# Twelve warm-up matmuls, later squares of x, and another order of low parts in a decoder step

## The chip, the cores and the metric

The kernel runs on one core of a Trainium2 chip. A core has a matrix engine (TensorE, PE in the profile; PEld is its weight load), a vector engine (VectorE, DVE), a scalar engine (ScalarE, ACT), a general engine (GpSimd, POOL) and an engine that issues transfers (SyncE, SP); ACT and POOL can issue transfers too. The metric is the device time of one execution in microseconds (us); less is better.

## What is computed

One layer of a decoder trunk, for 256 prompt tokens and 8 x 4 sample tokens (288 columns in all), 2048 channels, in float32:

```python
h = rmsnorm(x, norm1_g)
proj = einsum("btd,de->bte", h, w_in) + b_in
a, gate, z = proj[..., :1024], proj[..., 1024:2048], proj[..., 2048:]
u = a * sigmoid(gate)
c = silu(layernorm(depthwise_causal_conv(u_ext, conv_w, conv_b), ln_g, ln_b))   # 31 taps
d = multiscale_pool(z_ext, pos0)          # windows 2, 4, 8, 16; one for each group of 256 channels
p = einsum("btgc,gce->btge", d, pool_w).reshape(bsz, T, D_POOL) * pool_scale
x = x + einsum("btm,md->btd", concatenate([c, p]), w_out)
f = square(relu(einsum("btd,df->btf", rmsnorm(x, norm2_g), w_ff1)))            # 8192 wide
x = x + einsum("btf,fd->btd", f, w_ff2)
y = rmsnorm(x, norm_f)
```

The new histories of the convolution and of the pooling are outputs as well.

## The kernel before

Channels lie on the 128 partitions, the 288 tokens along the free dimension: `xT` is 16 tiles of 128 x 288. Each weight and each activation is split into a high part (rounded to the matmul's fp32r type) and a low part (what is left), and each product is made of three matmuls: high by high, low by high, high by low.

The weights come from memory as half-tiles of 128 x 1024 (`wr`, six buffers; loads on SP's queue). `split_part` rounds one on ACT to `whi` (line 274) and makes `wlo` in one of three ways: "V" is one subtraction on DVE (line 279); "G" is two subtractions of 128 x 512 on POOL (line 282); "D" writes the negated high part on ACT (line 276) and lets a DMA that POOL issues add the weights to it from memory (line 277). `WAYS` lists the way for each of the four half-tiles of a group of products, in order; "c3" is a convolution group, "p3" a pooling group (the third, of window 16). `whi` and `wlo` have five buffers each. The groups follow in the order of `SEQUENCE` (c0 and c1 together, c2, c3, c4, p3, c5, p2, and so on); a group is 96 matmuls.

The start is written out by hand. SP loads, for each pair of channel tiles, x and the weights of c0 and c1. `warm` is nine matmuls of a constant on TensorE (line 214) that nothing reads. `first_split(k0)` rounds the weights of one pair (`whi`, lines 363 and 370; low part on DVE, line 372) and makes the high parts of x times the norm's gain, `hx` (line 368 on ACT, 366 on DVE for the first; low parts on DVE, line 375). These conversions are traced for all eight pairs first; `squares()` is traced after them, inside the first product group, and fills the tile of `z_all`, which is still free: eight squares of a pair of tiles on ACT (line 417), added up on DVE in two sums (line 419), which are joined (lines 420 and 421).

The inverse root of the mean square isn't needed for the products, only to scale them afterwards. `rsqrt_sums` sums the squares over the partitions by small matmuls into `pt`, at a fixed place in TensorE's order (`between`: behind the low parts of the last pair), then takes roots on a 96 x 3 tile `st` (lines 249 to 256: DVE, one ACT root, DVE). `spread` turns them into a row on all partitions by six small matmul passes, also into `pt`, at a fixed place two tiles of channels into the product group c2 (`between={2: first_rows}`). A MEMSET of `z_all` on POOL (line 534) waits until the small matmuls have read the sums. After that come the scaling of the products, the convolution on DVE (line 460), and all else.

The order on each engine comes from a scheduler that places instructions, by the order in which they were traced and by a simulated time, when the program is built; each engine then works strictly in that order. `tc.issue_after(i)` makes what is traced inside it come behind `i` on that engine and adds no wait.

Of the kernel before, what the change touches and what calls it, by code (L numbers as in the profile page):

```python
# [11 lines left out]
AF = mybir.ActivationFunctionType  # L12
# [57 lines left out]
TURN = "110100" * 4 + "01" * 6 + "1100" * 3  # L70


WAYS = {"c2": "GVGV", "c3": "GDGG", "c4": "GDGD", "p3": "GDDG", "c5": "GDGD", "c": "GGGV", "p": "GVVG", "w0": "VV", "w": "GG", "ff": "VV"}


VEC = (("norm1_g", 16), ("b_in", 24), ("conv_b", 8), ("ln_g", 8), ("ln_b", 8), ("pool_scale", 8), ("norm2_g", 16), ("norm_f", 16))
# [10 lines left out]
def trunk_kernel(ctx: ExitStack, tc: tile.TileContext, io):  # L87
# [3 lines left out]
    nc = tc.nc  # L91
# [32 lines left out]
    def act2(name, **kw):  # L124

        return rows(actp.tile([P, 4, T], F32R, name=nm(name), **(kw or {"tag": "act"})))
# [4 lines left out]
    def ms(name):  # L131
        return msp.tile([P, 2, 512], F32, name=nm(name), tag="ms")

    def f32(t):
        return t.bitcast(F32)
# [15 lines left out]
    xT = const.tile([P, KT, T], F32, name="xT")  # L151
# [4 lines left out]
    def v(key, j):  # L156
        return vec[:, OFF[key] + j : OFF[key] + j + 1]
# [24 lines left out]
    def by_pair(t):  # L182
        return t[:].rearrange("p (i k) c -> p i k c", i=2)
# [26 lines left out]

    load_table(AF.Sqrt, ones[:, 0:1])
    warm = ms("warm")
    for j in range(9):
        nc.tensor.matmul(warm[:, 0, 0:P], ones, ones, start=True, stop=True)
    ident = const.tile([TB, TB], F32, name="ident", padded_shape=[TB, TB + 40])
    make_identity(nc, ident)
# [51 lines left out]
    def split_part(raw, src, hi, lo, way):  # L268

        nc.scalar.copy(hi, raw)  # L274
        if way == "D":
            nc.scalar.activation(lo, f32(hi), AF.Copy, scale=-1.0)
            nc.gpsimd.dma_start(lo, src, accum_op=ALU.add)
        elif way == "V":
            nc.vector.tensor_tensor(lo, raw, f32(hi), op=ALU.subtract)  # L279
        else:  # L280
            for j in range(0, raw.shape[1], 2):
                nc.gpsimd.tensor_tensor(lo[:, j : j + 2, :], raw[:, j : j + 2, :], f32(hi[:, j : j + 2, :]), op=ALU.subtract)  # L282

    def spl():
        return [wspl.tile([P, 4, 256], F32R, name=nm("w" + part), tag="w" + part) for part in ("hi", "lo")]
# [4 lines left out]
    def split(halves, stage="ff"):  # L290

        parts = []
        for raw, src in halves:
            turns[stage] = turns.get(stage, -1) + 1
            parts.append(spl())
            ways = WAYS.get(stage) or WAYS[stage[0]]
            split_part(raw, src, *parts[-1], ways[turns[stage] % len(ways)])
# [53 lines left out]
    def halves(x2):  # L351

        return [(x2[0][:, m, :], x2[1][:, m, :]) for m in range(2)]


    hx, firsts = [], []

    def first_split(k0):
        firsts.append([by_pair(t) for t in spl()])
        raw, hi, lo = raws[k0 // 2], *firsts[k0 // 2]  # L360
        blocks = [slice(i, i + 1) for i in range(2)] if k0 < 4 else [slice(0, 2)]
        hx.extend(halves(act2("hx")))
        nc.scalar.copy(hi[:, blocks[0]], raw[:, blocks[0]])  # L363
        for k in range(k0, k0 + 2):
            if k == 0:
                nc.vector.tensor_scalar(hx[k][0], xT[:, k, :], v("norm1_g", k), None, op0=ALU.mult)  # L366
            else:
                nc.scalar.activation(hx[k][0], xT[:, k, :], AF.Copy, scale=v("norm1_g", k))  # L368
        for b in blocks[1:]:
            nc.scalar.copy(hi[:, b], raw[:, b])  # L370
        for b in blocks:
            nc.vector.tensor_tensor(lo[:, b], raw[:, b], f32(hi[:, b]), op=ALU.subtract)  # L372
        for k in (k0 + 1, k0):
            hh, hl = hx[k]
            nc.vector.scalar_tensor_tensor(out=hl, in0=xT[:, k, :], scalar=v("norm1_g", k), in1=f32(hh), op0=ALU.mult, op1=ALU.subtract)  # L375

    for k in range(0, KT, 2):
        if k >= 12:
            first_load(k)
        first_split(k)  # L380
# [29 lines left out]
    def squares():  # L410

        nc.scalar.copy(scratch[:, :, :, 0:1], f32(firsts[2][0])[:, 1, 1, 0:10].rearrange("p (n k t) -> p n k t", n=5, t=1))
        for q in range(8):
            xq = xT[:, 2 * q : 2 * q + 2, :]
            a = q // 4
            dst = scratch[:, 2 + q % 3] if q % 4 else tot[a]
            nc.scalar.activation(dst, xq, AF.Square)
            if q % 4:
                nc.vector.tensor_tensor(tot[a], tot[a], dst, op=ALU.add)
        nc.vector.tensor_tensor(tot[0], tot[0], tot[1], op=ALU.add)  # L420
        nc.vector.tensor_tensor(tot[0][:, 0, :], tot[0][:, 0, :], tot[0][:, 1, :], op=ALU.add)
        return [tot[0][:, 0, :]]
# [100 lines left out]
    def first_sums():  # L523
        diag.append(rsqrt_sums(squares(), 1.0 / D, AF.Sigmoid))
        return diag[0][2]
# [96 lines left out]
    for g in range(8):  # L622
# [17 lines left out]
        for m, (ah, al) in enumerate(a2):  # L640
            k = 2 * g + m
# [29 lines left out]
    for ch in range(DFF // FCH):  # L671
# [19 lines left out]
        for g in range(8):  # L691
# [5 lines left out]
            for m in range(2):  # L697
                k = 2 * g + m
# [103 lines left out]
```

## Time and profile before

| | us |
|---|---|
| median of 3 runs (lowest to highest) | 1083.59 (1083.45 to 1083.73) |
| the profiled execution's own time | 1083.32 |
| its span, first to last instruction | 1081.2 |
| TensorE busy | 1069.8 |
| DVE busy | 636.8 |
| ACT busy | 477.6 |
| POOL busy | 174.6 |

The profile is of one execution. The span is shorter than the time of that execution by 2.1 us, which lie around it. Rows of the order of time read: start in us, duration in us, engine, line, operation, tile written and tiles read, shapes, count; in brackets the engine's idle time before and what ended it. Rows of waits read: who waited, for whom, us in total, times, longest.

### The profile page before, as it was taken

The numbers are of one execution on the slowest core, as the hardware profiler recorded it, in microseconds if no ns is written. First come the engines' busy times: TensorE is split into PE (matmuls) and PEld (weight loads), VectorE is DVE, ScalarE is ACT, GpSimd is POOL, SyncE is SP. The second block draws the span as 40 slices with busy tenths as digits, with TensorE's granted clock in tenths as the row PEclk, the third lists the DMA queues.
The fourth block names the chain that finished last, engine by engine and source line by source line (L and its number), as shares of the span: only waits on it lengthen the run. The fifth ranks groups of instructions, "written<-read, shape, count | busy, mean of one in ns | idle before, by whom it ended". The sixth has DMA issues, their size and how long they took to land.

```text
span 1081.2 us, 19573 instructions
## 1 busy us (share of the span) xinstructions
PE 1069.8 (99%) x8198; PEld 1068.7 (99%) x8198; DVE 636.8 (59%) x818; ACT 477.6 (44%) x585; POOL 174.6 (16%) x180
## 2 busy tenths in 40 slices
PE   9999999999999999999999999999999999999996
PEld 9999999999999999999999999999999999999996
DVE  7899999787754544444554444555544445554553
ACT  8654445565544433334443333444433334444441
POOL 0878979512000000000000000000000000000001
PEclk9999999999999999999999999999999999999998
DMA  9896468555555555555555555555555555555522
GB/s 327 281 272 184 140 187 250 172 170 170 166 173 164 171 173 165 170 171 164 172 173 162 172 168 168 171 173 163 173 170 165 172 173 163 172 170 165 172 79 88
DMA packets 58296, 190.71 MB, mean 176 GB/s; under 512 B 6240, under 2 KB 11232, under 8 KB 58208
## 3 DMA queue, kind: packets, MB, share of 16 engines
q1 hardware_dynamic: 56336, 184.35, 54.5%
q0 software_dynamic: 1008, 3.67, 1.9%
q8 instruction: 64, 1.05, 0.4%
q10 hardware_dynamic: 864, 1.44, 0.4%
q14 instruction: 24, 0.20, 0.1%
HBM read 185.16 MB, written 4.28 MB: 175 GB/s over the span
## 4 chain that ended last, share of the span: by engine, by line
PE 76%; issue 20%; DMA 2%; DVE 1%; ACT 0%; POOL 0%; SPq 0%; POOLq 0%; DVEq 0%
PE ac L305 75%; DMA wr<-in_w 1%; PE pp L305 1%; DMA u_all<-in_hist_c 0%; DVE wlo L279 0%; POOL xT L738 0%; PE pt L305 0%; ACT whi L363 0%; DVE hx L375 0%; DVE st L255 0%; DVE wlo L372 0%; PE pmean L305 0%; ACT hx L368 0%; SPq L191 0%; POOLq L788 0%
## 5 line engine op out<-in xcount | busy, mean ns | idle before, releaser
L274 ACT CAST whi<-wr 128x1024 fp32r<-128x1024 f32 (+1 forms) x332 | 346.5, 1044 | 553.6 <-PE ac L305 540.6
L279 DVE TENSOR_TENSOR wlo<-wr,whi 128x1024 fp32r<-128x1024 f32 x288 | 353.6, 1228 | 346.0 <-ACT whi L274 346.0
L305 PE MATMUL ac<-ax,whi 128*128 128x288 f32 x2048 | 351.0, 292 | 0.0
L305 PE MATMUL ac<-fx,whi 128*128 128x288 f32 x2048 | 350.2, 292 | 0.0
L305 PEld LDWEIGHTS ac<-ax,whi 128*128 128x128 f32 x2048 | 296.0, 187 | 0.0
L305 PEld LDWEIGHTS ac<-fx,whi 128*128 128x128 f32 x2048 | 295.6, 187 | 0.0
L305 PE MATMUL ac<-ax,wlo 128*128 128x288 f32 x1024 | 217.3, 292 | 0.0
L305 PE MATMUL ac<-fx,wlo 128*128 128x288 f32 x1024 | 216.4, 292 | 0.0
L305 PEld LDWEIGHTS ac<-ax,wlo 128*128 128x128 f32 x1024 | 162.6, 187 | 0.0
L305 PEld LDWEIGHTS ac<-fx,wlo 128*128 128x128 f32 x1024 | 162.2, 187 | 0.0
L305 PE MATMUL ac<-hx,whi 128*128 128x288 f32 x768 | 131.1, 294 | 1.4 <-DVE hx L366 1.4
L738 POOL TENSOR_TENSOR xT<-xT,rf 128x288 f32<-128x288 f32 x4 | 3.1, 796 | 800.1 <-ACT rf L742 800.1
L305 PEld LDWEIGHTS ac<-hx,whi 128*128 128x128 f32 x768 | 111.8, 189 | 1.6 <-ACT hx L368 1.6
L282 POOL TENSOR_TENSOR wlo<-wr,whi 128x512 fp32r<-128x512 f32 x74 | 101.5, 1420 | 35.7 <-ACT whi L274 34.6
L460 DVE SCALAR_TENSOR_TENSOR pc<-u_all,vec,pc 128x256 f32<-128x256 f32 x232 | 99.4, 481 | 1.9 <-ACT pc L457 0.7
L305 PE MATMUL ac<-hx,wlo 128*128 128x288 f32 x384 | 80.1, 294 | 0.0
L305 PEld LDWEIGHTS ac<-hx,wlo 128*128 128x128 f32 x384 | 60.9, 189 | 0.1
L305 PE MATMUL ac<-dx,whi 128*128 128x288 f32 x256 | 46.9, 294 | 0.0
L305 PE MATMUL ac<-mx,whi 128*128 128x288 f32 x256 | 44.6, 292 | 0.0
L682 DVE SCALAR_TENSOR_TENSOR t<-ac,r 128x576 f32<-128x576 f32 x32 | 24.2, 758 | 25.3 <-PE ac L305 25.3
L305 PEld LDWEIGHTS ac<-dx,whi 128*128 128x128 f32 x256 | 38.4, 188 | 0.1
L305 PEld LDWEIGHTS ac<-mx,whi 128*128 128x128 f32 x256 | 37.4, 187 | 0.0
(133 smaller groups left out, 535.2 us busy)
## 6 DMA issues: line engine op xcount, KB each, us to landing
wr<-in_w SPq DMA_DIRECT2D x335, 512.0 KB, 3.8
wlo<-in_w POOLq DMA_DIRECT2D x7, 512.0 KB, 8.2
xT<-in_xT SPq DMA_DIRECT2D x8, 288.0 KB, 7.7
wr<-in_w SPq DMA_DIRECT2D x5, 256.0 KB, 3.7
out_u_out<-u_all SPq DMA_DIRECT2D x1, 1208.0 KB, 9.1
u_all<-in_hist_c SPq DMA_DIRECT2D x8, 136.0 KB, 5.2
out_z_out<-z_all SPq DMA_DIRECT2D x1, 668.0 KB, 9.9
z_all<-in_hist_p SPq DMA_DIRECT2D x4, 152.0 KB, 6.9
```

Of the source, the lines that this page charges most:

```text
L274: nc.scalar.copy(hi, raw)
L279: nc.vector.tensor_tensor(lo, raw, f32(hi), op=ALU.subtract)
L282: nc.gpsimd.tensor_tensor(lo[:, j : j + 2, :], raw[:, j : j + 2, :], f32(hi[:, j : j + 2, :]), op=ALU.subtract)
L305: last = nc.tensor.matmul(*args, **kw)
L460: nc.vector.scalar_tensor_tensor(out=dst, in0=up[:, w : w + SEQ], scalar=cwv[:, w : w + 1], in1=pc, op0=ALU.mult, op1=ALU.add)
L682: nc.vector.scalar_tensor_tensor(out=t, in0=bk[:, :, :T], scalar=0.0, in1=both(rows2[0]), op0=ALU.max, op1=ALU.mult)
L738: eng.tensor_tensor(xk, xk, r[:, None, :].to_broadcast([P, n, T]), op=ALU.mult)
```

## The change

Three edits. Twelve warm-up matmuls instead of nine. The activations that make `hx` for the tiles 1 to 15 are kept in a list, and each square is issued behind one of them: the squares of pairs 0 to 3 behind tile 9's, that of pair 4 behind tile 11's, of pair 5 behind tile 13's, of pairs 6 and 7 behind tile 15's. In the pooling group of window 16 the third half-tile's low part is made on POOL and the fourth's by the accumulating DMA, where it was the other way round.

```diff
-WAYS = {"c2": "GVGV", "c3": "GDGG", "c4": "GDGD", "p3": "GDDG", "c5": "GDGD", "c": "GGGV", "p": "GVVG", "w0": "VV", "w": "GG", "ff": "VV"}
+WAYS = {"c2": "GVGV", "c3": "GDGG", "c4": "GDGD", "p3": "GDGD", "c5": "GDGD", "c": "GGGV", "p": "GVVG", "w0": "VV", "w": "GG", "ff": "VV"}
...
-    for j in range(9):
+    for j in range(12):
         nc.tensor.matmul(warm[:, 0, 0:P], ones, ones, start=True, stop=True)
...
-    hx, firsts = [], []
+    hx, firsts, scaled = [], [], []
...
-                nc.scalar.activation(hx[k][0], xT[:, k, :], AF.Copy, scale=v("norm1_g", k))
+                scaled.append(nc.scalar.activation(hx[k][0], xT[:, k, :], AF.Copy, scale=v("norm1_g", k)))
...
-            nc.scalar.activation(dst, xq, AF.Square)
+            with tc.issue_after(scaled[2 * min(max(q + 1, 4), 7)].ins):
+                nc.scalar.activation(dst, xq, AF.Square)
```

## The prediction

> **What bounds the kernel now.** I read the page first, then TensorE's waits, its pace by stretches, and last the instructions of the first 36 us in order of time with the chain of waits beside them.
>
> ```profile
> span 1081.2 us, 19573 instructions
> PE 1069.8 (99%) x8198; PEld 1068.7 (99%) x8198; DVE 636.8 (59%) x818; ACT 477.6 (44%) x585; POOL 174.6 (16%) x180
> ```
>
> TensorE (PE) is busy for 1069.8 of 1081.2 us, so only what moves its first and its few idle moments can move the end. The list of its waits is short:
>
> ```profile
> PE ac L305 <- DVE hx L366: 1.4, 1, 1.4
> PE warm L214 <- DVE cst L229: 1.0, 1, 1.0
> ```
>
> ```profile
> PEld pt L305 <- DVE st L256: 0.3, 1, 0.3
> ```
>
> The warm-ups start at 1.0 us, there is a hole of 1.4 us ahead of the first real product, and 0.3 us are lost where the weight load of the tile `pt` (the spreading of the inverse roots) waits for the vector engine (DVE). Those are the idle moments; the rest is pace, in this table of stretches (stretch, length, TensorE busy, instructions):
>
> ```profile
> 6.60:9.68 3.08, 3.07 (x13) 1.00 1.05 407
> 9.68:30.00 20.32, 20.32 (x156) 1.00 1.01 363
> ```
>
> The same 288-column product comes every 237 ns (3.08/13) at first, and every 130 ns (20.32/156) after 9.68 us. The view's clock column says 1.00 in both, so the pace shows the slow clock and the column doesn't.
>
> From 30 to 36 us the order of time reads:
>
> ```profile
> 27.90 3.95 POOL L282 TENSOR_TENSOR wlo<-wr,whi 128x512 fp32r<-128x512 f32 x2 [25.59 <-ACT whi L274]
> ...
> 28.48 0.75 DVE L420 TENSOR_TENSOR z_all<-z_all 128x576 f32<-128x576 f32 x1
> ...
> 29.27 1.43 DVE L421 TENSOR_TENSOR z_all<-z_all 128x288 f32<-128x288 f32 x1
> ...
> 30.63 2.31 DVE L279 TENSOR_TENSOR wlo<-wr,whi 128x1024 fp32r<-128x1024 f32 x1
> ...
> 32.22 0.59 PE L305 MATMUL pt<-ones,z_all 128*96 128x1 f32 x6
> 32.53 0.20 POOL L534 MEMSET z_all<- 128x120 f32 x1 [0.68 <-PE pt L305]
> ...
> 32.69 2.65 POOL L282 TENSOR_TENSOR wlo<-wr,whi 128x512 fp32r<-128x512 f32 x2
> 32.86 0.15 DVE L249 TENSOR_SCALAR st<-pt 96x3 f32<-96x3 f32 x1
> ...
> 33.49 0.61 DVE L254 TENSOR_TENSOR st<-st 96x3 f32<-96x3 f32 x1
> ...
> 34.14 1.22 DVE L255 SCALAR_TENSOR_TENSOR st<-st 96x3 f32<-96x3 f32 x1
> 35.39 0.16 DVE L256 SCALAR_TENSOR_TENSOR st<-st 96x3 f32<-96x3 f32 x1
> ...
> 35.61 0.91 PE L305 MATMUL pt<-ident,st 96*128 96x96 f32 x6
> ```
>
> The last sum of squares (L421) ends at 30.70 and TensorE takes it only at 32.22: 1.5 us of slack there. But the three-column arithmetic behind it (L249 to L256) begins at 32.86, when the half-tile subtraction L279 ends, and lasts to 35.55; TensorE is there 0.3 us before. DVE and GpSimd (POOL) take turns: L255 works on 96x3 elements, takes 1.22 us, and ends at 35.36, when POOL's two subtractions end (32.69 + 2.65 = 35.34); L421 and L279 are stretched while POOL's earlier pair (27.90 to 31.85) runs. The chain of waits passes through the same rows, not through TensorE. So up to 35.6 us the end is set by DVE and POOL; TensorE is a close second.
>
> The Trainium skill, page "SBUF — State Buffer", section "Who interferes with whom", says that a DVE instruction with two SBUF inputs and a GpSimd one that reads SBUF exclude each other for the whole instruction. The trace agrees (L255, 1.22 us, ends with POOL). By that rule a TensorE that runs ahead gains nothing here: the spreading stays at 35.6 us.
>
> **The change part by part.**
>
> ```profile
> 1.04 4.21 PE L214 MATMUL warm<-ones 128*128 128x128 f32 x18 [1.04 <-DVE cst L229]
> ...
> 6.61 1.30 PE L305 MATMUL ac<-hx,whi 128*128 128x288 f32 x4 [1.36 <-DVE hx L366]
> ...
> 10.05 0.61 ACT L370 CAST whi<-wr 128x512 fp32r<-128x512 f32 x1
> ...
> 10.73 1.76 PE L305 MATMUL ac<-hx,whi 128*128 128x288 f32 x12
> ...
> 13.59 2.41 ACT L417 ACTIVATE z_all<-xT 128x576 f32<-128x576 f32 x4
> ...
> 14.88 2.49 DVE L419 TENSOR_TENSOR z_all<-z_all 128x576 f32<-128x576 f32 x3 [0.17 <-ACT z_all L417]
> ...
> 15.90 1.04 ACT L363 CAST whi<-wr 128x1024 fp32r<-128x1024 f32 x1
> ...
> 17.29 1.22 DVE L372 TENSOR_TENSOR wlo<-wr,whi 128x1024 fp32r<-128x1024 f32 x1
> ...
> 18.68 1.21 PE L305 MATMUL ac<-hx,wlo 128*128 128x288 f32 x8
> ...
> 25.84 1.04 ACT L363 CAST whi<-wr 128x1024 fp32r<-128x1024 f32 x1
> ...
> 27.35 1.22 DVE L372 TENSOR_TENSOR wlo<-wr,whi 128x1024 fp32r<-128x1024 f32 x1
> ```
>
> Warm-ups. Nine are 18 passes in 4.21 us, 0.234 us each; three more are six passes, 1.4 us, so they end at 6.65 where nine ended at 5.25. The first real product waits for DVE until 6.61. Cost: 0 to 0.04 us, and I take 0. Their gain: TensorE works almost without a hole from 1.04 on. At best the slow pace is over before 6.61: 13 products at 130 instead of 237 ns are 1.4 us. Not all of it can be kept: the second block of the next pair's weights is rounded until 10.66 (L370), its products were due at 10.73 + 8 x 0.13 = 11.8 (four of the 12 close the pair before, four use the first block), so the lead is cut to 11.8 - 10.7 = 1.1 us. At worst the pace changes at 9.68 as now, lead 0. The pace changed 3.1 us after the hole's end, and the new stretch without hole is over 5 us long by 6.61, so I am nearer the upper end: a lead of 1.1 us after pair two.
>
> The Trainium skill, page "TensorE: Matmul & The Clock Gate", section "What's actually happening", has the clock released by a busy window of about 3.4 us at a free-running phase. The trace agrees as far as it goes (slow for 3.1 us after a hole of 1.4 us). By that rule, as an estimate, the release falls between 4.5 and 7.9 us with twelve warm-ups, and if TensorE alone counted the time would be 1083.32 - 1.1 = 1082.2 us.
>
> Squares. Four squares (L417, 2.41 us) run on ScalarE (ACT) from 13.59 to 16.0, ahead of the rounding of the weights of channels 6 and 7 (15.90). Their low half is ready at 17.29 + 1.22 = 18.51 and used at 18.68: 0.17 us of slack, so without the move the lead would be lost here. Behind the change the rounding can start when its weights land:
>
> ```profile
> L187 SPq DMA_DIRECT2D wr<-in_w x1: 614/614/614, 5.4 to 5.4; - x1
> ...
> DMA to landing us min/median/max: 8.1/8.1/8.1
> ```
>
> That is 5.4 + 8.1 = 13.5, so it moves 2.3 us forward and its low half on DVE to 14.7, ready by 15.9, against a use at 18.68 - 1.1 = 17.6. The four squares run at about 15.4 to 17.7, and each conversion up to channels 14 and 15 comes one square (0.6 us) sooner, since one square fewer stands before it. Two squares then stand together before the last rounding, which stays at 25.84: the same ACT work lies before it. DVE is without idle time from 14.88; its work up to L420 is the same, with the additions behind instead of before the first low half. What is bought: the 0.17 us in the row of 14.88, at most; what can be lost: about 0.1 us for each addition that follows directly on another (2.49 us for three, 0.83 each; a single one at 0.75). I take -0.1 us, between -0.2 and +0.4. The DMA queues issue the same transfers in the same order; what SyncE (SP) issues behind a buffer's release comes 0 to 2.3 us sooner, into a DMA system already at 1.01 of its 16 engines in the table, so I count nothing for it.
>
> Third pooling group. Its third half-tile goes from the accumulating DMA to POOL, its fourth from POOL to the DMA. No instruction is added.
>
> ```profile
> 65.94 0.88 POOL L277 DMA_DIRECT2D wlo<-in_w  x1
> 68.78 0.87 POOL L277 DMA_DIRECT2D wlo<-in_w  x1 [1.96 <-ACT wlo L276]
> 70.64 2.54 POOL L282 TENSOR_TENSOR wlo<-wr,whi 128x512 fp32r<-128x512 f32 x2 [0.99 <-ACT whi L274]
> ```
>
> ```profile
> 69.50 1.05 ACT L274 CAST whi<-wr 128x1024 fp32r<-128x1024 f32 x1 [0.29 <-issue]
> ```
>
> The first fence is POOL's order of time, the second ACT's, the next the landing of the transfer of 68.78, the last TensorE's.
>
> ```profile
> DMA to landing us min/median/max: 10.0/10.0/10.0
> ```
>
> ```profile
> 78.36 0.68 PE L305 MATMUL ac<-hx,whi 128*128 128x288 f32 x4
> 78.88 0.52 PE L305 MATMUL ac<-hx,wlo 128*128 128x288 f32 x2
> ```
>
> The transfer issued at 68.78 lands at 78.8, and the products with that low part start at 78.88 though two steps of 0.13 us behind 78.49 would be due at 78.75: 0.1 us lost. On POOL that half takes 2.54 us from about 67.5 (3.1 us, 24 products, before the fourth's 70.64), eight us early. The fourth half is due 3.1 us behind the third, at 82.0; its DMA can issue at about 71.7 (rounding from 69.5, two ACT steps of 1.05, as in the third half) and lands at 81.7 even with the longest delay seen. Gain 0.1 us; bounds: 0.1 us gain, and a loss of 0.5 us if its landing slips by another microsecond. The raw tile of the third half is held 2.6 us longer, that of the fourth given back as much sooner; two loads on SP's queue change by that, for weights of the group after next.
>
> The sum, against the profiled execution's own 1083.32 us: the lead of 1.1 us stops at the spreading (0); the DVE chain -0.1; the pooling group -0.1; 1083.1 us. That execution lies 0.27 us under the median of 1083.59, so against the median this is -0.5 us, -0.04%, inside the 0.2% (2.2 us) that a measurement of this kernel can tell from no change.
>
> **The rivals.** (1) The lead goes through. The scheduler writes each engine's order anew; if L279 comes behind L249 to L256, these start when `pt` ends, 32.81 - 1.1 = 31.7, and last without POOL's turns about 1.6 us (2.7 less the 0.5 and 1.05 us by which L254 and L255 exceed 0.16). TensorE then binds: 1.1 + 0.3 + 0.1, or 1081.9; half of it, 1082.6, where one POOL turn stays. For it: L421 is ready at 30.70, before TensorE's new 31.1. Against: L279's inputs are ready long before, and it fills DVE's wait for `pt`. (2) The sums come late. Each square has a fixed earliest place now, and none by which it must be done. If four of them fall behind the rounding at 25.84 and two more roundings after it, the last ends near 32, L421 near 34, `pt` at 34.6, and the arithmetic with POOL's two turns (which wait for `pt` through the MEMSET) ends near 37.5 instead of 35.55: 1085.2, and 1086 or more with a DMA late behind it. It decides from where L421 ends after 31.1. For it: the squares stand behind all conversions in the program. Against: in the trace one fits after each conversion. (3) The pace doesn't change sooner: the lead is 0, the spreading is at 35.5 all the same, 1083.1 to 1083.3; it can't be told from the forecast by the time.
>
> **How the numbers follow.** Forecast together with (3): 0.55, with its own range 1082.8 to 1083.7 (+-0.4 of the DVE chain, 0.1 of the pooling group, and the 0.27 between profile and median). (1): 0.27, 1081.9 to 1082.8, and 0.02 of it beyond 0.2%. (2): 0.18, 1083.8 to 1086.5, a third of it beyond 1085.8. The range 1081.9 to 1085.0 leaves out 0.02 below and about 0.1 above. Faster by over 0.2%: 0.02; slower: 0.06; the same: 0.92.
>
> **What would show it.** Warm-ups: 24 passes, and the stretch 6.60 to 9.68 with more than 13 products. Squares: the rounding of 15.90 near 13.6, four squares behind 15.4, L420 still near 28.4. Spreading: TensorE's wait for L256 grown from 0.3 to over 1 us with its start at 35.4 to 35.6 is the forecast; a start at 34.2 and no wait is (1); a wait at `pt` for L421 is (2). Pooling group: no 0.1 us before the low part at 78.8. A new TensorE wait anywhere after 40 us, or a reordering on DVE around L279, would make the forecast wrong.

## The result and the profile after

| | before | after |
|---|---|---|
| median of 11 runs, us (lowest to highest) | 1083.73 (1082.75 to 1084.17) | 1085.98 (1084.88 to 1087.34) |
| ratio, 95% interval | | 1.0022 (1.0014 to 1.0029) |
| the profiled execution, us | 1083.32 | 1085.98 |

The kernel became slower by 0.22%. The forecast was 1083.1 us, no measurable difference; the measured time lies 1.0 us above the upper end of its range. From the page of the changed kernel, then TensorE's list of waits (who, for whom, us in total, times, longest):

```profile
span 1084.1 us, 19586 instructions
...
PE 1070.7 (99%) x8204; PEld 1068.6 (99%) x8204; DVE 638.6 (59%) x818; ACT 477.0 (44%) x585; POOL 175.4 (16%) x180
```

```profile
...
PE pp L305 <- ACT dx L502: 0.7, 1, 0.7
PE pp L305 <- DVE dx L503: 0.5, 1, 0.5
PE ac L305 <- DVE u_all L449: 0.4, 1, 0.4
PE pt L305 <- DVE st L256: 0.2, 1, 0.2
PE pt L305 <- DVE z_all L422: 0.2, 1, 0.2
```

Left out are the holes at the start, 1.2 and 1.0 us, and 0.2 us at the end. The first three shown are new: 1.6 us of TensorE idle (line numbers behind 417 are one higher than before). The last, 0.2 us for the sums, is new too and lies at the start. TensorE's order of time shows where:

```profile
159.68 0.42 PE L305 MATMUL ac<-hx,whi 128*128 128x288 f32 x2
160.77 0.54 PE L305 MATMUL pp<-dx,whi 128*128 128x288 f32 x2 [0.66 <-ACT dx L502]
...
162.11 0.80 PE L305 MATMUL pp<-dx,whi 128*128 128x288 f32 x4 [0.54 <-DVE dx L503]
...
173.42 0.37 PE L305 MATMUL ac<-dx,whi 128*128 128x288 f32 x1 [0.41 <-DVE u_all L449]
```

`pp` are the products of the pooling group p1, `dx` is its input, split into high and low parts. That is 125 us behind the start that the squares edit touches. The list counts from the modelled end of the product before; from the start of one product to the start of the next, the three waits cost 0.8, 0.7 and 0.6 us above a step of 0.13 us, 2.1 us in all. The table of stretches counts TensorE's products; first two rows of before, then the same two of after:

```profile
60.00:80.00 20.00, 20.00 (x155) 1.00 1.00 275
...
150.00:175.00 25.00, 25.00 (x194) 1.00 0.85 235
```

```profile
60.00:80.00 20.00, 19.92 (x150) 1.00 0.99 271
...
150.00:175.00 25.00, 23.39 (x174) 1.00 0.76 207
```

Twenty products at 0.13 us are missing around the three waits (2.6 us), and five from 60 to 80 us (0.65 us; behind a hole of 0.1 us at 62.7 us, where the weight load waits for an accumulating DMA, products come every 133.3 ns instead of 130.0). The start gained 0.8 us in these two profiles (the spreading at 34.82 against 35.61). That sums to 2.5 us, where the spans differ by 2.9.

At the start the change did what it says. After, in order of time, and the first of the two stretches that the prediction had shown of before:

```profile
1.04 4.33 PE L214 MATMUL warm<-ones 128*128 128x128 f32 x24 [1.04 <-DVE cst L229]
...
12.81 1.05 ACT L363 CAST whi<-wr 128x1024 fp32r<-128x1024 f32 x1
...
14.63 2.40 ACT L418 ACTIVATE z_all<-xT 128x576 f32<-128x576 f32 x4
...
29.59 1.43 DVE L422 TENSOR_TENSOR z_all<-z_all 128x288 f32<-128x288 f32 x1
30.94 1.21 DVE L279 TENSOR_TENSOR wlo<-wr,whi 128x1024 fp32r<-128x1024 f32 x1
...
34.82 0.91 PE L305 MATMUL pt<-ident,st 96*128 96x96 f32 x6 [0.25 <-DVE st L256]
```

```profile
6.60:9.68 3.08, 3.08 (x24) 1.00 1.06 407
```

Twenty-four products instead of 13 from 6.60 to 9.68: the slow pace was over before the first real product. The rounding of the weights of channels 6 and 7 is at 12.81 instead of 15.90, the four squares follow at 14.63. Nothing there is late.

### The profile page after: what moved, and what is told of

Its sections match the earlier page's. It is cut to its first block, busy times and chain, and to the rows that moved or that the text cites. A ratio compares the mean times of both kernels' runs of the same rounds, so it can differ in the third digit from the quotient of the medians.

```text
span 1084.1 us, 19586 instructions
## 1 busy us (share of the span) xinstructions
PE 1070.7 (99%) x8204; PEld 1068.6 (99%) x8204; DVE 638.6 (59%) x818; ACT 477.0 (44%) x585; POOL 175.4 (16%) x180
## 3 DMA queue, kind: packets, MB, share of 16 engines
q8 instruction: 64, 1.05, 0.4%
## 4 chain that ended last, share of the span: by engine, by line
PE 66%; issue 21%; DVE 6%; POOL 4%; DMA 2%; ACT 1%; POOLq 0%; SPq 0%; DVEq 0%
PE ac L305 66%; DVE pc L461 3%; POOL wlo L282 2%; POOL s L492 1%; DMA wr<-in_w 1%; DMA wlo<-in_w 1%; DVE wlo L279 1%; POOL prd L464 0%; ACT z_all L418 0%; DVE d L497 0%; ACT hx L368 0%; DVE c L466 0%; ACT whi L363 0%; DVE dx L503 0%; POOL xT L739 0%
## 5 line engine op out<-in xcount | busy, mean ns | idle before, releaser
L279 DVE TENSOR_TENSOR wlo<-wr,whi 128x1024 fp32r<-128x1024 f32 x288 | 352.8, 1225 | 346.2 <-ACT whi L274 346.2
L282 POOL TENSOR_TENSOR wlo<-wr,whi 128x512 fp32r<-128x512 f32 x74 | 102.2, 1431 | 33.8 <-ACT whi L274 33.7
L461 DVE SCALAR_TENSOR_TENSOR pc<-u_all,vec,pc 128x256 f32<-128x256 f32 x232 | 99.1, 481 | 3.5 <-ACT pc L458 2.6
```

Of the source, the lines that this page charges most:

```text
L461: nc.vector.scalar_tensor_tensor(out=dst, in0=up[:, w : w + SEQ], scalar=cwv[:, w : w + 1], in1=pc, op0=ALU.mult, op1=ALU.add)
```

## The experiments

All ratios are to the kernel before, run on the same chip. The kernels came in five groups; before measured 1083.16 us beside e1 to e4, 1083.47 beside e5 to e8, 1083.38 beside e9 to e12, 1083.33 beside e13 to e16, and 1083.35 beside e17 and e18.

### Which edit, and by what: e1 to e4

The program's written orders, compared: the warm-ups change only TensorE's own first rows, the swap of low parts a few places on ACT and POOL, but the squares edit gives DVE, ACT, POOL and SP another order from 36 to about 165 us too. e1, e2 and e3 make one edit each; e4 makes all three and holds those four engines behind 36 us to the order that they have without the squares edit, by edges without a wait (lists cut):

```diff
+    keep = {
+        "DVE": "645 646 677 647 648 718",
...
+    }
+    traced = {i.name: i for i in nc.cur_bb.bb.instructions}
+    for order in keep.values():
+        order = [traced["I-" + n] for n in order.split()]
+        for first, then in zip(order, order[1:]):
+            tc.add_manual_dep(then, first.name, mybir.DependencyInfo(mybir.DependencyClass.NoSync, mybir.DependencyReason.DATA), reason="keep")
```

> The later squares alone, nine warm-ups, old order of the third pooling group's low parts. Before, on the same chip, is about 1083.7 us. Theory A (the later squares shift the scheduler's simulated times, so that DVE, ACT and POOL get another order behind 36 us, and TensorE waits at 160 to 173 us): 1085 to 1087 us, with waits of about 0.5 to 1 us at 160 and at 173 us. Theory B (TensorE, 0.8 us ahead, runs into low parts and pooling results that are not ready): no lead without the early clock, 1083.3 to 1084.2 us and none of those waits. Theory C (the exchanged low parts cost it): 1083.3 to 1084.2 us.

> Twelve warm-ups alone. Its order on every engine but TensorE is that of before. All three theories: no 2 us loss. Theories A and C: 1083.0 to 1083.8 us, as the lead is lost where the low part for channels 6 and 7 is ready only at 18.5 us, and none of the waits at 160 to 173 us. Theory B: if any lead lives past 36 us, waits of that size at 160 to 173 us, up to 1084.5 us.

> The exchanged low parts of the third pooling group alone. Theories A and B: 1083.4 to 1083.8 us, TensorE's 0.1 us before the low part at 78.8 us gone. Theory C: 1085 us or more, with TensorE waits behind 60 us.

> All three edits, but DVE, ACT, POOL and SP are held to the order of before behind the start (from about 36 us on; the start up to there is that of the changed kernel). Theory A: the lead of 0.8 us at the spreading stays and the waits at 160 to 173 us go: 1082.4 to 1083.3 us, faster than before. Theory B: the lead is the same, so are the waits: 1085 to 1087 us. Theory C: 1085 us or more.

| kernel | median, us | ratio (95%) |
|---|---|---|
| e1, squares alone | 1085.97 | 1.0031 (1.0019 to 1.0042) |
| e2, warm-ups alone | 1082.73 | 0.9995 (0.9986 to 1.0004) |
| e3, low parts alone | 1083.38 | 1.0001 (0.9992 to 1.0010) |
| e4, all three, old order behind 36 us | 1083.12 | 0.9998 (0.9989 to 1.0007) |

The squares edit carries the loss, and the order that it brings behind 36 us carries it: with that held, the waits at 159 to 173 us are gone. e2 came out 0.3 us below what was expected: its profile loses only 0.2 us at the low part for channels 6 and 7. e4 wasn't faster than before although the start was in its profile; its pace gives a reason (e8 below).

### Is the order enough, and which part: e5 to e8

e5 is before with the new order behind 36 us. e6 and e7 are the changed kernel with a part held: e6 from 100 us, e7 from 36 to 100 us. e8 is e4 with one more edit:

```diff
-            conv_pair(i, conv_products(i, classes=TURN if i == 5 else "", **(dict(gets=ahead(1), between={12: lambda: pool_products(1)}) if i == 7 else {})))
+            conv_pair(i, conv_products(i, classes=TURN if i in (4, 5) else "", **(dict(gets=ahead(1), between={12: lambda: pool_products(1)}) if i == 7 else {})))
```

> The kernel before with none of the three edits, but with DVE, ACT, POOL and SP behind 36 us held to the order in which the scheduler wrote them for the squares-only kernel. Theory A (the order behind the start costs the 2 to 3 us, the squares' own place costs nothing): 1085 to 1086.5 us, and TensorE waits of some 0.9, 0.8 and 0.7 us near 159, 160.5 and 172 us. Rival (the squares at their new places cost it, through a later start or a transfer that they push): 1083 us as before, no such waits. Squares stay at 13.6 to 16 us either way.

> All three edits, with only the order behind about 100 us held to that of the kernel without the squares edit; from 36 to 100 us the scheduler's new order stays. If the order of the second pooling group's chain on DVE, behind 100 us, is what is late (theory A, narrowed): no TensorE waits at 159 to 173 us and 1082.3 to 1083.4 us. Rival (DVE falls behind between 36 and 100 us, through the taps put ahead of pooling steps there): the waits stay, 1085 to 1086 us. It also has no wait near 50 us if the early place of the accumulating transfer's issue is what avoids it, and so TensorE's fast pace until 60 us.

> All three edits, with only the order from 36 to 100 us held to the old one; behind 100 us the order is what the scheduler then gives, which is neither of the two others. If the late order decides and this one is like the squares kernel's: 1084.5 to 1086 us with waits at 159 to 173 us. If the early order decides: 1082.5 to 1083.5 us, no such waits. A wait of 0.2 us near 50 us, as with all held.

> All three edits with the whole order behind 36 us held to the old one, and the product classes of group c4 taken in the turning order that c5 has. If a short TensorE wait flips the pace from 130.0 to 133.3 ns a product and the turning order flips it back: 130 ns from about 60 us on instead of 133.3 until 84 us, that is 0.5 to 0.7 us less than with the old classes, 1082.4 to 1082.7 us. Rival (the slow pace of those stretches belongs to the groups, or to chance): 133.3 ns until 84 us again and 1083.1 us. If the turning order makes c4 wait for its low parts, a new wait near 62 us and up to 0.5 us more.

e5: 1085.79 us, 1.0023 (1.0013 to 1.0032), with the waits. The order alone is enough. Where the squares stand costs nothing that can be told (e4 has them late).

e6: 1086.17 us, 1.0024 (1.0013 to 1.0034), against the expectation. But its waits are others. The longest in TensorE's list, then the order of time on POOL and DVE:

```profile
PE ac L305 <- DVE dx L515: 1.3, 1, 1.3
```

```profile
162.78 3.53 POOL L282 TENSOR_TENSOR wlo<-wr,whi 128x512 fp32r<-128x512 f32 x2 [0.30 <-ACT whi L274]
166.28 0.34 POOL L500 TENSOR_TENSOR d<-s,z_all 128x64 f32<-128x64 f32 x1
167.35 0.76 DVE L503 TENSOR_TENSOR dx<-d,dx 128x576 fp32r<-128x576 f32 x1 [2.22 <-ACT dx L502]
```

The old order was held on POOL only up to the instruction before L500 of the last pooling group. Left free, that one fell behind two subtractions of 3.5 us. e16, below, tests this.

e7: 1084.41 us, 1.0010 (1.0001 to 1.0019), between what the two theories gave. It has no wait at 159 us, but the order that the scheduler then gave has one of 0.2 us at 110 us, and behind it TensorE's slower pace: 480 products from 108 to 172 us where e4 and e8 have 494. This third order tells little about the first two.

e8: 1082.71 us, 0.9992 (0.9983 to 1.0001). Pace of e4, then of e8, by the same stretch:

```profile
48.00:84.00 36.00, 36.00 (x272) 1.00 0.93 253
```

```profile
48.00:84.00 36.00, 36.00 (x277) 1.00 0.93 253
```

Five products more in 36 us, 0.65 us. e4's steps are 133.3 ns long behind a short wait at 50 us and until the group that has the turning order, 130.0 ns elsewhere; in e8 c4 has that order and the pace is back from 66 us on. The medians differ less clearly than the profiles: both intervals hold 1.0.

### A theory that fell: two steps of ACT, e9 to e11

Between 36 and 60 us DVE waits longer for ACT in the new order. e5's list of DVE's waits from 36 to 60 us:

```profile
DVE u_all L448 <- ACT tg L446: 2.2, 1, 2.2
DVE pc L460 <- ACT pc L457: 1.7, 2, 1.0
```

Before has 1.2 and 0.7 there. ACT does the negated high part of c3's second half ahead of the sigmoids `tg`, and two conversions ahead of `pc`. I took these 1.9 us for the source of the lateness at 158 us, since it is as large. e9 puts both back in the changed kernel, e10 the first alone, e11 puts both forward in before; all other places are held.

```diff
 ACT, e9 and e10:
-round, negate, tg, tg
+round, tg, tg, negate
 ACT, e9 alone, in two places:
-round, pc
+pc, round
```

> All three edits and the order of the changed kernel on every engine, except for two places on ACT: the negated high part of c3's second half stands behind the two sigmoids of c2 again (with its accumulating transfer behind POOL's two products prd, as before), and two conversions stand behind the first taps' ACT step pc again instead of ahead of it. Theory A2 (DVE's waits for ACT between 36 and 60 us grow from 2.5 to 4.4 us through these two, DVE has no idle time to make that up in, and the second pooling group's chain is 1.9 us late at 158 us): DVE's waits there back to about 2.5 us, no TensorE waits of 0.7 to 1 us at 159 to 173 us, 1082.3 to 1083.5 us. Rival (DVE's own new order behind 44 us costs it): waits stay, 1085 to 1086 us.

> As the kernel with both steps put back, but only the negation (and its transfer) is moved back; the two conversions stay ahead of pc. By theory A2 DVE's waits from 36 to 60 us are about 3.2 us (4.4 less 1.1), the chain at 158 us is 0.7 us late instead of 1.9, and as the first wait of 0.95 us came from a lateness of 1.9 about 1.0 of it is slack: no wait or one under 0.3 us at 159 us, 1082.5 to 1084.3 us. If the negation isn't the larger part: 1085 us and more.

> The kernel before with its own order on every engine and none of the three edits, except that the negation (with its transfer) is put ahead of the sigmoids and the two conversions ahead of pc. Theory A2: these alone are enough, DVE's waits from 36 to 60 us grow to about 4.4 us, TensorE waits of some 0.7 to 1 us come up at 159 to 173 us, 1084.8 to 1086 us. Rival (it takes DVE's new order too): 1083 to 1084 us and no such waits.

e9: 1085.59 us, 1.0020 (1.0012 to 1.0029). e10: 1085.65 us, 1.0022 (1.0013 to 1.0031). e11: 1083.70 us, 1.0004 (0.9995 to 1.0012). The theory falls on all three: back, they mend nothing; forward, they cost nothing. In e11 DVE does wait 2.2 and 1.2 us there, and TensorE has no wait behind it. The equal size was chance.

### A version with the two harmless edits: e12

```diff
-    for j in range(9):
+    for j in range(12):
...
-classes=TURN if i == 5 else ""
+classes=TURN if i in (4, 5) else ""
```

> The kernel before with twelve warm-up matmuls and the turning order of the product classes in c4 as well as in c5; squares and low parts as before. No TensorE wait at 159 to 173 us; 130 ns a product wherever the kernel with the warm-ups alone has it. Expected 1082.4 to 1082.8 us, that is no more than 0.1 us from the warm-ups alone, since that profile shows no slow stretch before 84 us; if the unprofiled executions often have the wait near 79 us that the profile before has, 0.1 to 0.3 us less.

1083.26 us, 1.0000 (0.9991 to 1.0009); 0.5 us above what was expected. TensorE in its profile, in order of time:

```profile
16.84 1.33 PE L305 MATMUL ac<-hx,whi 128*128 128x288 f32 x8 [0.22 <-ACT whi L363]
18.40 0.81 PE L305 MATMUL ac<-hx,wlo 128*128 128x288 f32 x4 [0.23 <-DVE wlo L372]
```

Without the squares edit TensorE, when it runs ahead, waits for the weights of channels 6 and 7. That is the wait that the squares edit takes away.

### Where DVE meets POOL: e13 to e16

Before and after are level at 117.7 us, where both start the same subtraction on DVE (117.80 and 117.67). Twenty us on, after is 3.2 us behind. DVE and POOL of before, in order of time (d, dx: inputs of the pooling group p2; L279 and L282: the low parts of weights on DVE and on POOL; tz: the start of p1's chain):

```profile
127.70 0.69 DVE L496 SCALAR_TENSOR_TENSOR d<-s,z_all 128x512 f32<-128x512 f32 x1 [0.96 <-POOL s L495]
...
129.25 2.21 POOL L463 TENSOR_TENSOR prd<-u_all,vec 128x992 f32<-128x992 f32 x1
...
131.08 1.00 DVE L502 TENSOR_TENSOR dx<-d,dx 128x576 fp32r<-128x576 f32 x1
...
135.88 1.22 DVE L279 TENSOR_TENSOR wlo<-wr,whi 128x1024 fp32r<-128x1024 f32 x1
...
137.80 0.75 DVE L482 TENSOR_TENSOR tz<-ac,rb 128x576 f32<-128x576 f32 x1
138.01 2.54 POOL L282 TENSOR_TENSOR wlo<-wr,whi 128x512 fp32r<-128x512 f32 x2 [2.47 <-ACT whi L274]
```

And after:

```profile
124.68 3.00 POOL L282 TENSOR_TENSOR wlo<-wr,whi 128x512 fp32r<-128x512 f32 x2
124.77 1.75 DVE L497 SCALAR_TENSOR_TENSOR d<-s,z_all 128x512 f32<-128x512 f32 x1 [1.16 <-POOL s L496]
...
130.19 2.21 POOL L464 TENSOR_TENSOR prd<-u_all,vec 128x992 f32<-128x992 f32 x1 [1.24 <-DVE u_all L449]
130.42 2.60 DVE L503 TENSOR_TENSOR dx<-d,dx 128x576 fp32r<-128x576 f32 x1
...
137.91 3.52 POOL L282 TENSOR_TENSOR wlo<-wr,whi 128x512 fp32r<-128x512 f32 x2 [2.50 <-ACT whi L274]
138.77 1.51 DVE L279 TENSOR_TENSOR wlo<-wr,whi 128x1024 fp32r<-128x1024 f32 x1
140.99 0.74 DVE L483 TENSOR_TENSOR tz<-ac,rb 128x576 f32<-128x576 f32 x1
```

DVE's `d` is 1.06 us longer beside POOL's subtractions, `dx` 1.6 us longer, since it meets POOL's `prd` from its start and not only in its last 0.4 us. There is no more work in them. `d` and `dx` read two tensors in SBUF. The Trainium skill, page "SBUF — State Buffer", section "Who interferes with whom", says that such a DVE instruction and a GpSimd one that reads SBUF exclude each other, and that issue order decides who blocks. The traces agree: `dx` ends 0.62 us behind the end of `prd` in after (133.02 against 132.40) and in before (132.08 against 131.46) alike. Another `dx` of the same size, with POOL idle beside it, takes 0.74 us (at 161.31 us in after).

e13 moves `dx` alone, behind five taps. e14 also gives the 11 DVE instructions ahead of it and POOL's division `s` and sum the old places. e15 puts those new places into before. e16 is e6 with the old order held to about 200 us. (tap: one multiply-add of the convolution, L461; scale: products times the inverse root, L445; subtract: a low part of weights, L279 or L282.)

```diff
 DVE, e13 and e14:
-dx, tap, tap, tap, tap, tap
+tap, tap, tap, tap, tap, dx
 DVE, e14:
-d, tap, scale, tap, subtract, scale, tap, tap, u_all, u_all, tap
+tap, tap, tap, scale, tap, scale, subtract, tap, d, u_all, u_all
 POOL, e14:
-s, s, sum_c, divide, subtract, subtract
+sum_c, s, s, subtract, subtract, divide
```

> All three edits and the changed kernel's order everywhere, except for one DVE instruction: the subtraction dx of the pooling group p2 (at 130.4 us, 2.6 us long beside POOL's prd) stands behind the next five taps. Theory A3 (DVE loses 2.7 us between 117 and 155 us because three kinds of its two-input instructions meet POOL's): dx takes 0.7 to 1.0 us, the chain of the next pooling group comes 1.6 us sooner, of TensorE's waits at 159 to 173 us (0.82, 0.71 and 0.58 us above a step) at most 0.3 us in all is left, 1082.8 to 1084.0 us. Rival (the taps' own order costs it): all waits stay, 1085.5 to 1086.5 us.

> As the kernel with dx moved, and besides d, the taps around it and POOL's last division s of that group in the old order, in all 12 DVE and 3 POOL places between 120 and 134 us. Theory A3: d back from 1.75 to 0.7 us, dx at 1.0, no TensorE wait at 159 to 173 us, 1082.3 to 1083.5 us. Rival (the loss is spread over the whole new order, of which this stretch is a tenth): waits of 0.3 us and more stay, 1084.5 us or more.

> The kernel before, none of the three edits, its own order on every engine except for those 12 DVE and 3 POOL places between 120 and 134 us, which have the changed kernel's order. Theory A3: d 1.75 and dx 2.6 us, the three TensorE waits at 159 to 173 us come up, 1084.8 to 1086.3 us. Rival (it takes the rest of the new order too): 1083 to 1084 us, waits under 0.3 us.

> As the kernel with the order behind 100 us held, which had kept its 1086 us, with the hold reaching to about 200 us instead of 163 on POOL: there the second of the two pieces of d of the last pooling group had come behind two subtractions (3.5 us), and TensorE waited 1.5 us for it at 168 us. Theory A3: that one place explains e6, no TensorE wait at 159 to 173 us, 1082.3 to 1083.5 us. Rival (the new order from 36 to 100 us costs it): 1085 us and more.

e15: 1086.73 us, 1.0030 (1.0018 to 1.0041): these places alone, in a kernel with none of the edits, bring the whole loss. They bring it partly by another way than was expected: `d` takes 1.75 us, but `dx` 1.79 and not 2.6, and DVE waits 1.1 us longer for POOL's `s` ahead of `d` and 0.7 us for ACT's cast ahead of `dx`.

e16: 1083.90 us, 1.0002 (0.9993 to 1.0011), 0.4 us above its range: the old order from 100 us on takes the loss away to within what can be told. e6's wait of 1.3 us is gone, which fits that one POOL instruction as its cause; e16 holds other places behind 163 us as well. Its profile keeps two waits of 0.3 us, one for a low part at 69 us and one for `u_all` at 171.6 us.

But e13, 1085.06 us, 1.0017 (1.0008 to 1.0026), and e14, 1085.24 us, 1.0017 (1.0008 to 1.0026), missed: TensorE's waits were as long as before the mending. In e13 `dx` met POOL's next pair and still took 1.48 us. In e14 DVE only changed what it waited for (DVE's and POOL's order of time):

```profile
130.75 1.66 DVE L461 SCALAR_TENSOR_TENSOR pc<-u_all,vec,pc 128x256 f32<-128x256 f32 x4 [2.11 <-ACT pc L458]
...
137.12 3.52 POOL L282 TENSOR_TENSOR wlo<-wr,whi 128x512 fp32r<-128x512 f32 x2 [3.89 <-ACT whi L274]
137.65 1.84 DVE L279 TENSOR_TENSOR wlo<-wr,whi 128x1024 fp32r<-128x1024 f32 x1
```

In the new order ACT casts `dx` and rounds weights ahead of `pc`. The last two rows show the rest. POOL's pair starts at a time that TensorE sets (it waits for ACT's rounding, and ACT for TensorE to give the buffer back; in every kernel of the table it starts 0.07 us behind the start of the last two products of p2). Worked out from the order of time, with POOL's pair and DVE's second subtraction of p0 (the one two taps ahead of tz):

| kernel | POOL's pair starts | DVE's subtraction | its end against the pair's start |
|---|---|---|---|
| before | 138.01 | 135.88 to 137.10 | -0.91 |
| e16 | 138.19 | 136.97 to 138.18 | -0.01 |
| after | 137.91 | 138.77 to 140.28 | +2.37 |
| e1 | 137.10 | 138.02 to 139.47 | +2.37 |
| e9 | 138.01 | 138.84 to 140.37 | +2.36 |
| e13 | 136.97 | 137.43 to 139.34 | +2.37 |
| e14 | 137.12 | 137.65 to 139.49 | +2.37 |
| e15 | 137.35 | 138.47 to 139.72 | +2.37 |

Where DVE comes first it is done before POOL starts, in e16 by a hair. Where POOL comes first, DVE waits for POOL's first half (1.27 us) and ends 2.37 us behind the pair's start, whether it arrived 0.46 us (e13) or 1.12 us (e15) into that half. So e13 and e14, which made DVE come earlier but not early enough, moved nothing.

The profiles of all the kernels divide the same way. Eight have 2.36 to 2.38 us (e5 and e10 beside the six above), and all eight have the two waits of `pp` at 159 to 162 us. Eleven lie between -1.75 and -0.01 us, and none of them has these two waits. The twentieth is e18, below. The third wait, for `u_all` at 172 us, isn't tied to this alone: e6 and e16 come first and keep 0.4 and 0.3 us of it.

### The gate: e17 and e18

e17 is e14 with ACT's three steps in the old order as well. e18 is before with the subtraction ahead of it done twice more (same result).

```diff
 ACT, e17:
-cast dx, round, pc
+round, pc, cast dx
```

```diff
             split_part(raw, src, *parts[-1], ways[turns[stage] % len(ways)])
+            if (stage, turns[stage]) == ("p0", 1):
+                for again in range(2):
+                    nc.vector.tensor_tensor(parts[-1][1], raw, f32(parts[-1][0]), op=ALU.subtract)
```

> As the kernel with the whole stretch of 120 to 134 us in the old order on DVE and POOL, and besides ACT's three steps of that stretch in the old order (pc ahead of the cast of dx). Theory A4 (all that counts is whether DVE gets to the second p0 subtraction before POOL's pair starts, some 22 us ahead of the products pp of p1): no wait of DVE for pc, that subtraction done before POOL's pair starts, tz about 3 us earlier, no TensorE wait over 0.3 us at 159 to 173 us, 1082.5 to 1083.7 us. Rival (the loss is spread over the new order): the waits stay, 1085 us.

> The kernel before, none of the three edits, its own order; after the first of the two DVE subtractions of p0 (133.2 us) the same subtraction is done twice more (2.3 us of DVE, same result). Theory A4: DVE meets POOL's pair, the second subtraction ends not 2.3 but about 3.3 us late, tz starts 18.8 us ahead of TensorE's stop as in the slow kernels, and TensorE's first step at 159 us is the same 0.95 us as there, the second 0.83 us; 1084.8 to 1086.3 us. Rival (lateness just adds up): tz 2.3 us late; of the 2.0 us by which the cast of dx is ahead of its use, 0.3 us are lacking, so a first step of 0.4 us; 1084 to 1085 us.

e17: 1082.63 us, 0.9993 (0.9985 to 1.0002). Its order of time, then all of TensorE's waits:

```profile
129.89 1.08 DVE L503 TENSOR_TENSOR dx<-d,dx 128x576 fp32r<-128x576 f32 x1
...
135.08 1.21 DVE L279 TENSOR_TENSOR wlo<-wr,whi 128x1024 fp32r<-128x1024 f32 x1
136.71 2.54 POOL L282 TENSOR_TENSOR wlo<-wr,whi 128x512 fp32r<-128x512 f32 x2 [2.35 <-ACT whi L274]
137.00 0.75 DVE L483 TENSOR_TENSOR tz<-ac,rb 128x576 f32<-128x576 f32 x1
```

```profile
PE warm L214 <- DVE cst L229: 1.0, 1, 1.0
PE ac L305 <- DVE hx L366: 0.3, 1, 0.3
PE pt L305 <- DVE st L256: 0.2, 1, 0.2
PE ends L731 <- DVE cst L236: 0.2, 1, 0.2
```

The subtraction is done 0.42 us before POOL's pair starts, and the waits are gone: all three edits, with a few places of one 14-us stretch put back, run as fast as before. e8, e17 and e2 lie lowest against before (0.9992, 0.9993 and 0.9995), some 0.3% under the changed kernel; from the kernel before their intervals don't tell them apart.

e18: 1087.58 us, 1.0041 (1.0027 to 1.0054), more than either theory gave. Its order of time (lines behind 300 are three higher than in before):

```profile
133.96 3.46 DVE L300 TENSOR_TENSOR wlo<-wr,whi 128x1024 fp32r<-128x1024 f32 x2
...
137.58 2.54 POOL L282 TENSOR_TENSOR wlo<-wr,whi 128x512 fp32r<-128x512 f32 x2 [2.51 <-ACT whi L274]
138.90 2.30 DVE L279 TENSOR_TENSOR wlo<-wr,whi 128x1024 fp32r<-128x1024 f32 x1
...
161.95 0.85 PE L308 MATMUL pp<-dx,whi 128*128 128x288 f32 x2 [2.18 <-ACT dx L504]
```

The two repeats took 3.46 us, since they met POOL's pair before. DVE then came 1.32 us behind the start of the next pair, when its first half (1.27 us) was just over, waited for the second half, and ended 3.62 us behind the start: 1.25 us later than the others, one half of POOL's pair. So here the lateness went in steps of POOL's instructions and didn't just add up; the size that I had expected, one step, was wrong by the price of the repeats.

## Why the prediction was wrong

**The step that failed** is the one on the squares: "I take -0.1 us, between -0.2 and +0.4", counted over the first 36 us alone. It measured +2.8 us (e1 against 1083.16). The prediction costed what the squares move on ACT and DVE at the start, and held all that comes behind for unchanged. It had written the reason against this itself, in rival 1 ("The scheduler writes each engine's order anew"), but used it for one instruction, L279. What the runs showed in its place: the new order makes DVE late between 120 and 134 us, where `d` and `dx` meet POOL's instructions and DVE waits longer for POOL and ACT. The new places of 12 DVE and 3 POOL instructions are enough for that (e15), and putting them back mends it when three steps of ACT go back too (e17). DVE then comes to its second p0 subtraction behind POOL, and the chain of p1 reaches TensorE late. "A new TensorE wait anywhere after 40 us" was named as what would make the forecast wrong, without a chance or a price.

**The sentence on SP** ("I count nothing for it") stands as far as e15 can tell, which brings the whole loss with SP's old order; no run took SP's new order alone.

**Warm-ups.** Cost 0 was right. In the profile of after the passes ended at 5.37, not 6.65 (in e2's, 6.53): the slow pace was over before the last of them, the upper end of the prediction's bounds. e2 says that they gain 0.05% at the median, not told from nothing. The 1.1 us of lead was sized from a slow start that is rare here: of the seven profiles with nine warm-ups, only the one of before has 13 products from 6.60 to 9.68 us, and the six others (e1, e3, e5, e11, e15, e18) have 22 to 25 without any more warm-ups. "The lead stops at the spreading" was wrong in the profile of after: the spreading came at 34.82. But that place varies by itself. Five executions whose program is the old one up to 36 us (before, e5, e11, e15, e18) have it at 35.61, 35.02, 35.42, 34.82 and 35.40; their mean is 35.25, and the earliest is where after's is. So, as an estimate, 0.4 us of the 0.8 is the change's, and it may be none. POOL and DVE took turns as described (L255 lasts 1.22 us in both), only L279 ended sooner, 1.21 us long instead of 2.31, since POOL's pair was over when it began. So after's profile lies between the forecast and rival 1, about in the middle. Rival 1's own sum has a slip: 2.7 less 0.5 and 1.05 is 1.15 us, not 1.6, and 1083.32 less 1.5 is 1081.8. Nothing hangs on it, since TensorE binds there.

**The clock.** The first products run at the fast pace after nine warm-ups too (e5: four in 0.78 us from 6.54 on, where before took 1.30), though not in the profile of before. The Trainium skill, page "TensorE: Matmul & The Clock Gate", section "What's actually happening", says that the window is free-running and that the number of slow matmuls differs from run to run. These runs agree: 13 products in the stretch in one execution, at the fast pace in another with the same warm-ups.

**Rival 2**, late sums, named the right edit and nearly the right time (1085.2), by the wrong mechanism: L422 ended at 31.02, not 34, and TensorE lost 0.2 us there. The time came out by another way.

**Third pooling group.** -0.1 us was expected; e3 measures 1.0001 (0.9992 to 1.0010), which can't tell it. The 0.1 us of wait at 78.8 us is gone in the profile of after. (The prediction looked for it ahead of 78.88; four products from 78.36 on are due to end there. It shows in that row's own length, 0.52 us for two products instead of 0.42.)

**Still open:** why steps are 133.3 ns behind a short wait; whether the new order from 36 to 100 us costs anything by itself. e16 and e17 have it, at 1.0002 and 0.9993, so no cost can be told; but DVE's lead over POOL's pair, 0.91 us in before, is 0.01 us in e16 and 0.42 in e17.

## What to carry to other kernels

Where a scheduler places the instructions, price an edit by the orders of all engines that it gives, to the end of the program, and not by the stretch that the edit touches. Where two engines exclude each other, look at who gets there first and with how much to spare: a shift below the margin (0.91 us in before) cost nothing that could be told here, one above it cost the rest of an instruction of the other engine, and mending part of the shift mended nothing. Read a gain off more than one profile: the start that the warm-ups were to mend was slow in one of seven. Before taking an equal size for a cause (1.9 us of waits here, 1.9 us of lateness there), put back the suspected part alone.

## What the runs showed of the hardware

- DVE's `dx` took 2.60 us where it met POOL's `prd` from its start, 1.00 where it met the last 0.4 us of it, and 0.74 with POOL idle. DVE's low-part subtraction ended 2.37 us behind the start of POOL's pair in the six kernels of the table in which POOL came first, wherever in the first half it arrived.
- TensorE has two fast paces. Behind a short wait (0.06 us in e4, up to 0.7) a product often takes 133.3 instead of 130.0 ns, in e8 until the group with the turning order of its classes: 272 against 277 products in 36 us (e4, e8), 480 against 494 in 64 us (e7).
- A hole of 2.2 us put TensorE back to the slow pace: in e18 the 12 products behind it take 3.4 us (161.95 to 165.36), where 1.6 are due, with 0.4 us of waiting for `dx` among them. The view's clock column is 0.51 there; in the slow stretch at the start of before it stays at 1.00.
- The start differs by up to 0.8 us between executions of the same instructions, and by 1.35 us over all the kernels (the spreading from 34.48 to 35.83).
